# Low parts of weights and a norm's shift moved from GpSimd to VectorE in some stretches of a decoder trunk

## The chip, the cores and the metric

One core of a Trainium2 chip runs the whole kernel in one launch. The metric is device time in microseconds (us), the median of three runs.

## The reference

One inference step of a 4-layer decoder trunk, in float32, for two groups that share all weights: one prompt of 512 tokens and 8 sequences of 8 new tokens ("sample"). Layers 0 and 3 have a Conformer convolution as mixer, layer 1 a sparse attention with three branches, layer 2 a causal pooling; every layer ends in a gated feed-forward block with a 3-tap convolution.

```python
mod = silu(c) @ ada_w[i] + ada_b[i]; sh1, sc1, g1, sh2, sc2, g2 = split(mod, 6)
h = rms_norm(x, norm1_g[i]) * (1 + sc1) + sh1
x = x + g1 * mixer(h)                       # conv / attention / pooling
h = rms_norm(x, norm2_g[i]) * (1 + sc2) + sh2
x = x + g2 * conv_ffn(h)                    # 1024 -> 2 x 2816 -> 1024
```

## The kernel before, in words

Activations lie transposed: 128 of the 1024 features on the partitions, 8 such blocks (m), and two halves of the tokens (h), each 288 columns: 256 of the prompt and 32 of the sample. `x[h][q]` holds four blocks (q = 0, 1) of one half.

Every product runs in split precision. A weight block arrives by DMA in `raw` (128 x 2048); ScalarE writes its high part (a rounded copy, line 300 or 275), and another engine subtracts that from the raw weights to get the low part (line 305 or 276). TensorE then does three products per block: high by high (line 349), high weight by low activation (350), low weight by high activation (351). The activations of a norm, `h`, are split the same way (lines 640, 643, 650, 654).

The feed-forward blocks between the mixers are plain code: lines 275 and 276 split a whole weight block there, lines 357 to 360 are the products. What lies between two feed-forward blocks (the end of one, the norm, the mixer, the second norm, the start of the next) is a **flow**: a list of tasks, each with an engine, a duration, its dependencies, and counts of PSUM banks and slots. `Flow.run` is a list scheduler. At each step it takes, of all ready tasks, the one that can start earliest by the durations written in the code; ties go to the lower `prio`, then to the task that was added first. It issues the task at once, so the order of every engine's instructions is the order that it finds. A task may name two engines; the one on which it would end first is taken:

```python
e = min(range(len(eng)), key=lambda i: max(t, free.get(eng[i], 0.0)) + dur[i] + bias[i])
key = (max(t, free.get(eng[e], 0.0)), prio, n)
```

Here `t` is when the task's inputs are ready, `free` when the engine is. Nothing in it knows that VectorE and GpSimd may hinder each other.

There are five flows: layer 0 from the start (0 to about 330 us), the end of feed-forward 0 with the attention (about 630 to 1260), the end of feed-forward 1 with the pooling (about 1630 to 1760), the end of feed-forward 2 with layer 3's convolution (about 2130 to 2445), and the end of feed-forward 3 with the final norm (from about 2810). `Flow` is made with 18 slots, or with `slots=0` where `(l + 1) % 3 == 1`, which is the attention's flow (l = 0) and the last one (l = 3).

`w_tasks` adds the tasks that split a weight block in chunks of 512 columns: `hi` on ScalarE, `part` (line 305) on VectorE or GpSimd; after the last chunk it issues the load of the next block on SyncE's queue. It is called after the norm's tasks have been added.

`f_norm` works by half and by four blocks. For the sample's columns: `s_mul` (GpSimd, line 629), `s_rs` (VectorE, line 633), `s_add` (GpSimd, line 637: the shift), `s_hi` (ScalarE, line 640), `s_lo` (VectorE, line 643). For the prompt's, block by block: `p_mul` (VectorE, line 646), `p_hi` (ScalarE, line 650), `p_lo` (VectorE, line 654). Line 586 is the reciprocal of the norm's root on VectorE. Lines 498 to 500 are the residual `x + g * y`. `f_pool` has a shift of its own (line 1242) that the diff leaves alone.

Of the kernel before, what the change touches and what calls it, by code (L numbers as in the profile page):

```python
# [27 lines left out]
OP = mybir.AluOpType  # L28
# [73 lines left out]
class Flow:  # L102
# [5 lines left out]
    def __init__(self, banks=8, slots=18, warm=True):  # L108
        self.clock = dict(tick=0, warm=True, done=0.0) if warm else {}
        self.tasks = []  # L110
        self.banks, self.slots = banks, slots

    def add(self, eng, dur, fn, *deps, take=0, give=0, st=0, sg=0, prio=0, bias=(0, 0, 0)):


        if isinstance(eng, str):
            eng, dur = (eng,), (dur,)
        flat = []

        def walk(x):  # L120
            if isinstance(x, (list, tuple)):
                for y in x:
                    walk(y)
            elif x is not None:
                flat.append(x)
        walk(deps)
        self.tasks.append((eng, dur, fn, flat, (take, st), (give, sg), prio, bias))
        return len(self.tasks) - 1
# [64 lines left out]
class Trunk:  # L193
# [87 lines left out]
    def w_tasks(self, fl, tag, *deps, lo=("DVE", "POOL")):  # L281

        nc = self.nc
        n = self.nu
        self.nu += 1
        assert self.plan[n][0] == tag, (self.plan[n][0], tag)
        if n < self.ns:
            return (lambda: self.ws[n]), self.wt[n][1] if self.wt.get(n, (None,))[0] is fl else [None] * 4
        assert n == self.ns
        cs = range(0, self.plan[n][1], 512)  # L290
        self.ns += 1
        out, parts = [], set()
        a = None
        before = self.wt[n - 1][1] if self.wt.get(n - 1, (None,))[0] is fl else None

        def hi(c):
            if c == 0:
                self.ws[n] = self.wp.tile([128, 2, 2048], F32R, name="w", tag="w")
            sl = slice(c, min(c + 512, self.plan[n][1]))
            nc.scalar.activation(self.ws[n][:, 0, sl], self.raws[n][:, sl], AF.Copy)  # L300

        def part(c, eng):
            sl = slice(c, min(c + 512, self.plan[n][1]))
            w, r = self.ws[n], self.raws[n]
            self.eng(eng).tensor_tensor(w[:, 1, sl], r[:, sl], w[:, 0, sl], OP.subtract)  # L305
            parts.add(c)
            if len(parts) == len(cs):
                del self.raws[n]
                self.nr += 1
                self.w_dma()  # L310
        for c in cs:
            a = fl.add("ACT", 0.54, lambda c=c: hi(c), a, before, *[d(c) if callable(d) else d for d in deps])
            d = tuple({"DVE": 0.62, "POOL": 1.2}[e] for e in lo)
            out.append(fl.add(lo, d, (lambda e, c=c: part(c, e)) if len(lo) > 1 else (lambda c=c: part(c, lo[0])), a))
        out += out[-1:] * (4 - len(out))
        self.wt[n] = fl, out
        return (lambda: self.ws[n]), out
# [297 lines left out]
    def f_norm(self, fl, l, which, rs, ready, mdep=None):  # L615

        nc = self.nc
        B = self.modv(l, 3 * which)
        s0, S = self.f_scale(fl, l, which, mdep)
        t = {}  # L620
        self.hh, get = self.parts()

        def tt(h, q):
            if (h, q) not in t:
                t[h, q] = self.slot([128, 4, H], F32, name="nt")
            return t[h, q]

        def s_mul(h, q):
            nc.gpsimd.tensor_tensor(self.svq(tt(h, q)), self.svq(self.X[h][q]), self.bcq(S(), q, h), OP.mult)

        def s_rs(h, q):
            v = tt(h, q)[:, :, HP:H]
            nc.vector.tensor_tensor(v, v, rs[h][1]()[:, None, HP:H].to_broadcast([128, 4, H - HP]), OP.mult)

        def s_add(h, q):
            v = self.svq(tt(h, q))
            nc.gpsimd.tensor_tensor(v, v, self.bcq(B, q, h), OP.add)

        def s_hi(h, q):
            nc.scalar.activation(get(0, h, q)[:, :, HP:H], tt(h, q)[:, :, HP:H], AF.Copy)  # L640

        def s_lo(h, q):
            nc.vector.tensor_tensor(get(1, h, q)[:, :, HP:H], tt(h, q)[:, :, HP:H], get(0, h, q)[:, :, HP:H], OP.subtract)

        def p_mul(h, m):
            nc.vector.scalar_tensor_tensor(tt(h, m // 4)[:, m % 4, :HP], self.xv(h, m)[:, :HP], S()[:, m, 0:1],
                                           rs[h][1]()[:, :HP], op0=OP.mult, op1=OP.mult)

        def p_hi(h, m):
            nc.scalar.activation(get(0, h, m // 4)[:, m % 4, :HP], tt(h, m // 4)[:, m % 4, :HP], AF.Identity,  # L650
                                 bias=B[:, m, 0:1])

        def p_lo(h, m):
            nc.vector.scalar_tensor_tensor(get(1, h, m // 4)[:, m % 4, :HP], tt(h, m // 4)[:, m % 4, :HP], B[:, m, 0:1],
                                           get(0, h, m // 4)[:, m % 4, :HP], op0=OP.add, op1=OP.subtract)
        dep = {}
        for h in range(2):
            for q in range(2):
                ms = range(4 * q, 4 * q + 4)
                x = fl.add("POOL", 0.4, lambda h=h, q=q: s_mul(h, q), s0[q], [ready[h, m] for m in ms])  # L660
                x = fl.add("DVE", 0.25, lambda h=h, q=q: s_rs(h, q), x, rs[h][0])
                x = fl.add("POOL", 0.4, lambda h=h, q=q: s_add(h, q), x)
                a = fl.add("ACT", 0.25, lambda h=h, q=q: s_hi(h, q), x)
                b = fl.add("DVE", 0.2, lambda h=h, q=q: s_lo(h, q), a)
                for m in ms:
                    x = fl.add("DVE", 0.4, lambda h=h, m=m: p_mul(h, m), s0[m // 4], ready[h, m], rs[h][0])
                    x = fl.add("ACT", 0.41, lambda h=h, m=m: p_hi(h, m), x)
                    x = fl.add("DVE", 0.4, lambda h=h, m=m: p_lo(h, m), x)
                    dep[h, m] = [a, b, x]
        return dep  # L670
# [2076 lines left out]
```

## Time and profile before

| | us |
|---|---|
| median of three runs | 2862.21 |
| lowest, highest | 2859.83, 2865.05 |
| the profiled execution | 2859.49 |
| its span | 2857.7 |
| TensorE busy in it | 2754.8 |

TensorE's matmuls are named `pa`, `pb`, `pd` in the feed-forward blocks, `pc` where a norm's output is consumed first, `pd` also for a mixer's output projection, `pp` for the pooling's product, `adaps` for the modulation, `st` for the sums of a norm. Line 351 takes the low part of a weight, line 350 the low part of an activation.

### The profile page before, as it was taken

How to read it: one execution, taken by the hardware profiler on the slowest of the kernel's cores; microseconds unless marked ns; L12 is line 12 of the kernel's file. 1: busy time of each engine (PE TensorE's matmuls, PEld its weight loads, DVE VectorE, ACT ScalarE, POOL GpSimd, SP SyncE). 2: the span in 40 equal slices, each digit the busy share in tenths (PEclk: the TensorE clock that was granted, in tenths of full speed). 3: DMA queues.
4: the chain of work that ended last, by engine and by line, in shares of the span. 5: the costliest groups of instructions: out<-in, count | busy, mean ns of one | idle time of the engine just before them, and what ended most of it. 6: DMA issues, size and time to landing. Idle time of an engine off the chain costs nothing.

```text
span 2857.7 us, 50727 instructions
## 1 busy us (share of the span) xinstructions
PE 2754.8 (96%) x20677; PEld 2473.0 (87%) x20677; DVE 1598.2 (56%) x3437; ACT 978.8 (34%) x2094; POOL 505.8 (18%) x917
## 2 busy tenths in 40 slices
PE   7999999999999999989999979999999989999998
PEld 5667999999899656889999958999998758999997
DVE  5545644445736575464455686545557456645555
ACT  3124422222546565342222244222233134322223
POOL 2432200000434334010000052000003432000001
PEclk8999999999999999999999989999999999999999
DMA  8554243333443446224222269222233561222221
GB/s 313 174 172 171 89 148 145 136 133 133 147 155 134 138 155 234 88 97 148 97 89 74 97 198 139 74 89 89 83 111 115 163 236 45 85 78 89 89 76 64
DMA packets 105385, 363.88 MB, mean 127 GB/s; under 512 B 28128, under 2 KB 38272, under 8 KB 83904
## 3 DMA queue, kind: packets, MB, share of 16 engines
q1 hardware_dynamic: 97248, 344.50, 36.3%
q0 software_dynamic: 2816, 8.39, 0.9%
q10 hardware_dynamic: 5088, 7.74, 0.8%
q8 instruction: 163, 2.67, 0.4%
q14 instruction: 70, 0.57, 0.1%
HBM read 335.38 MB, written 22.80 MB: 125 GB/s over the span
## 4 chain that ended last, share of the span: by engine, by line
PE 86%; DVE 6%; DMA 4%; ACT 1%; issue 1%; SPq 1%; POOL 1%; ACTq 0%; DVEq 0%; POOLq 0%
PE pa L357 6%; PE pa L360 6%; PE pa L358 6%; PE pb L358 6%; PE pb L357 6%; PE pb L360 6%; PE pd L357 5%; PE pd L360 5%; PE pd L358 5%; PE pd L349 3%; PE pd L350 3%; PE pd L351 3%; PE adaps L421 2%; PE pts L953 2%; DMA ada<-in_ada_dram 2%; PE pc L350 2%
## 5 line engine op out<-in xcount | busy, mean ns | idle before, releaser
L276 DVE TENSOR_TENSOR w<-raw,w 128x2048 fp32r<-128x2048 f32 (+1 forms) x117 | 259.4, 2217 | 388.1 <-ACT w L275 388.1
L357 PE MATMUL pa<-h,w 128*128 128x288 f32 x1280 | 363.3, 299 | 5.6 <-ACT w L275 5.6
L358 PE MATMUL pa<-h,w 128*128 128x288 f32 x1280 | 360.4, 296 | 0.0
L358 PE MATMUL pb<-h,w 128*128 128x288 f32 x1216 | 341.6, 295 | 0.0
L357 PE MATMUL pb<-h,w 128*128 128x288 f32 x1216 | 341.5, 296 | 0.0
L357 PE MATMUL pd<-u,w 128*128 128x288 f32 x1152 | 323.5, 296 | 0.0
L358 PE MATMUL pd<-u,w 128*128 128x288 f32 x1152 | 322.9, 295 | 0.0
L740 POOL COPY so<-ab 128x2 f32<-128x2 f32 x88 | 17.0, 193 | 1518.5 <-ACT ab L710 1518.5
L275 ACT ACTIVATE w<-raw 128x2048 fp32r<-128x2048 f32 (+1 forms) x117 | 218.9, 1871 | 176.4 <-PE pd L360 176.4
L360 PE MATMUL pa<-h,w 128*128 128x288 f32 x1280 | 274.9, 296 | 1.0 <-DVE w L276 1.0
L357 PEld LDWEIGHTS pa<-h,w 128*128 128x128 f32 x1280 | 241.8, 189 | 24.3 <-issue 16.8
L360 PE MATMUL pb<-h,w 128*128 128x288 f32 x1216 | 259.8, 295 | 0.0
L360 PE MATMUL pd<-u,w 128*128 128x288 f32 x1152 | 247.0, 296 | 0.0
L358 PEld LDWEIGHTS pa<-h,w 128*128 128x128 f32 x1280 | 242.1, 189 | 0.0
L358 PEld LDWEIGHTS pb<-h,w 128*128 128x128 f32 x1216 | 229.0, 188 | 0.0
L357 PEld LDWEIGHTS pb<-h,w 128*128 128x128 f32 x1216 | 228.7, 188 | 0.0
L357 PEld LDWEIGHTS pd<-u,w 128*128 128x128 f32 x1152 | 216.8, 188 | 6.7 <-issue 6.7
L358 PEld LDWEIGHTS pd<-u,w 128*128 128x128 f32 x1152 | 216.8, 188 | 0.0
L498 DVE TENSOR_TENSOR rtmp<-pd,mod 128x32 f32<-128x32 f32 x368 | 68.5, 186 | 261.6 <-PE pd L360 174.9
L305 DVE TENSOR_TENSOR w<-raw,w 128x512 fp32r<-128x512 f32 (+1 forms) x203 | 166.2, 859 | 84.2 <-ACT w L300 83.4
L720 ACT ACTIVATE ab<-ab 128x576 f32<-128x576 f32 x88 | 60.4, 687 | 435.2 <-DVE ab L739 435.2
L360 PEld LDWEIGHTS pa<-h,w 128*128 128x128 f32 x1280 | 205.9, 189 | 1.5 <-DVE w L276 1.3
(359 smaller groups left out, 6502.6 us busy)
## 6 DMA issues: line engine op xcount, KB each, us to landing
raw<-in_w_dram SPq DMA_DIRECT2D x165, 1024.0 KB
ada<-in_ada_dram SPq DMA_DIRECT2D x192, 512.0 KB
xs<-ub SPq DMA_DIRECT2D x56, 270.0 KB
raw<-in_w_dram SPq DMA_DIRECT2D x16, 768.0 KB
x<-in_x_dram SPq DMA_DIRECT2D x8, 576.0 KB
xsp<-x SPq DMA_DIRECT2D x8, 576.0 KB
x<-xsp SPq DMA_DIRECT2D x8, 576.0 KB
out_wo_dram<-in_sw_dram SPq DMA_DIRECT2D x8, 512.0 KB
```

The lines of the kernel that those rows point to most:

```text
L275: nc.scalar.activation(w[:, 0, :width], r[:, :width], AF.Copy)
L276: self.lo_eng.tensor_tensor(w[:, 1, :width], r[:, :width], w[:, 0, :width], OP.subtract)
L305: self.eng(eng).tensor_tensor(w[:, 1, sl], r[:, sl], w[:, 0, sl], OP.subtract)
L349: nc.tensor.matmul(ps[:, :H], hi, mv(k, 0, h), start=first, stop=False)
L350: nc.tensor.matmul(ps[:, :H], hi, mv(k, 1, h), start=False, stop=False)
L351: nc.tensor.matmul(ps[:, :H], lo, mv(k, 0, h), start=False, stop=last)
L357: nc.tensor.matmul(ps[h][:, :H], hi, mv(k, 0, h), start=first, stop=False)
L358: nc.tensor.matmul(ps[h][:, :H], hi, mv(k, 1, h), start=False, stop=False)
L360: nc.tensor.matmul(ps[h][:, :H], lo, mv(k, 0, h), start=False, stop=last)
L421: nc.tensor.matmul(self.a_ps[32 * j:32 * j + 32, 0:N], self.cm[:, k, :], raw[j * N // 1024][:, j * N % 1024:j * N % 1024 + N], start=(k == ...
L498: nc.vector.tensor_tensor(t, self.sv(ps), self.bc(G, m, h), OP.mult)
L720: self.nc.scalar.activation(acc, acc, AF.Silu)
```

## The change

`Flow` gets a flag `busy`, true where `slots == 0`. In the other flows a low part is planned with 0.68 us on VectorE and 2.6 us on GpSimd in place of 0.62 and 1.2, and `s_add` of `f_norm` is a VectorE task of 0.28 us in place of a GpSimd task of 0.4.

```diff
+        self.busy = slots == 0
...
-            d = tuple({"DVE": 0.62, "POOL": 1.2}[e] for e in lo)
+            d = tuple(({"DVE": 0.62, "POOL": 1.2} if fl.busy else {"DVE": 0.68, "POOL": 2.6})[e] for e in lo)
...
-        def s_add(h, q):
+        def s_add(h, q, e):
             v = self.svq(tt(h, q))
-            nc.gpsimd.tensor_tensor(v, v, self.bcq(B, q, h), OP.add)
+            self.eng(e).tensor_tensor(v, v, self.bcq(B, q, h), OP.add)
...
-                x = fl.add("POOL", 0.4, lambda h=h, q=q: s_add(h, q), x)
+                e = "POOL" if fl.busy else "DVE"
+                x = fl.add(e, 0.4 if fl.busy else 0.28, lambda h=h, q=q, e=e: s_add(h, q, e), x)
```

## Rows read from the trace of the kernel before

**Rows 1.** The page's part 1: busy us (share of the span) xinstructions, by engine.

```profile
PE 2754.8 (96%) x20677; PEld 2473.0 (87%) x20677; DVE 1598.2 (56%) x3437; ACT 978.8 (34%) x2094; POOL 505.8 (18%) x917
```

**Rows 2.** Windows: length, busy us (xinstructions) by engine, PEclk, DMA share, GB/s.

```profile
1650.00:1760.00 110.00, 89.11 (x569) 63.59 (x567) 91.41 (x207) 49.52 (x116) 56.22 (x92) 0.91 0.92 169
...
2440.00:2800.00 360.00, 360.00 (x2716) 359.85 (x2716) 189.86 (x405) 98.77 (x154) 10.71 (x82) 1.00 0.24 83
```

**Rows 3.** Waits of PE, whole span: total us, times, longest us.

```profile
PE pc L350 <- DVE h L643: 9.1, 4, 3.7
```

**Rows 4.** Waits of PE, 240 to 330 us; 2400 to 2440 answers the same row.

```profile
PE pc L350 <- DVE h L654: 2.2, 2, 1.4
```

**Rows 5.** Lines 305, 637, 633: count, ns min/median/max; the POOL rows by flow.

```profile
L305 DVE TENSOR_TENSOR w<-raw,w x203: 559/685/2808, 23.6 to 2820.3; 128x512 fp32r<-128x512 f32 x101, 128x384 fp32r<-128x384 f32 x1
L305 POOL TENSOR_TENSOR w<-raw,w x14: 1266/1464/2245, 44.3 to 310.6; 128x512 fp32r<-128x512 f32 x14
L305 POOL TENSOR_TENSOR w<-raw,w x13: 1267/1299/1627, 1631.5 to 1727.7; 128x512 fp32r<-128x512 f32 x13
L305 POOL TENSOR_TENSOR w<-raw,w x20: 1262/1456/2218, 2129.2 to 2426.9; 128x512 fp32r<-128x512 f32 x20
L637 POOL TENSOR_TENSOR nt<-nt,mod x28: 418/528/593, 26.1 to 2432.9; 128x128 f32<-128x128 f32 x28
L633 DVE TENSOR_TENSOR nt<-nt,rstd x28: 275/279/1442, 25.5 to 2432.5; 128x128 f32<-128x128 f32 x28
```

**Rows 6.** Timeline of DVE from 2157 us (start us, us, engine line op xcount), layer 3's norm.

```profile
2157.92 1.43 DVE L633 TENSOR_TENSOR nt<-nt,rstd 128x128 f32<-128x128 f32 x1
2159.27 3.90 DVE L646 SCALAR_TENSOR_TENSOR nt<-x,nS,rstd 128x256 f32<-128x256 f32 x4
...
2164.37 1.24 DVE L500 TENSOR_TENSOR x<-x,rtmp 128x32 f32<-128x32 f32 x1
...
2166.13 0.28 DVE L643 TENSOR_TENSOR h<-nt,h 128x128 fp32r<-128x128 f32 x1
...
2184.41 0.86 DVE L646 SCALAR_TENSOR_TENSOR nt<-x,nS,rstd 128x256 f32<-128x256 f32 x2
```

**Rows 7.** Timeline of POOL in the same stretch.

```profile
2157.91 1.29 POOL L305 TENSOR_TENSOR w<-raw,w 128x512 fp32r<-128x512 f32 x1
...
2159.98 2.90 POOL L305 TENSOR_TENSOR w<-raw,w 128x512 fp32r<-128x512 f32 x2
```

**Rows 8.** Timeline of PE in the same stretch, idle before in brackets.

```profile
2166.46 0.61 PE L350 MATMUL pc<-h,w 128*128 128x288 f32 x1 [3.67 <-DVE h L643]
```

**Rows 9.** Windows: PE just after that wait, columns as in Rows 2.

```profile
2166.46:2169.47 3.01, 3.01 (x15) 2.73 (x19) 3.01 (x9) 2.21 (x5) 1.76 (x3) 0.50 0.99 280
```

**Rows 10.** Timeline of DVE, then of POOL, 295 to 302 us: layer 0's second norm.

```profile
296.43 2.46 DVE L646 SCALAR_TENSOR_TENSOR nt<-x,nS,rstd 128x256 f32<-128x256 f32 x3
298.81 1.37 DVE L643 TENSOR_TENSOR h<-nt,h 128x128 fp32r<-128x128 f32 x1
300.11 1.49 DVE L646 SCALAR_TENSOR_TENSOR nt<-x,nS,rstd 128x256 f32<-128x256 f32 x1
...
297.13 4.18 POOL L305 TENSOR_TENSOR w<-raw,w 128x512 fp32r<-128x512 f32 x3
```

**Rows 11.** Timelines of ACT, DVE and POOL in the pooling flow.

```profile
1659.02 1.16 ACT L300 ACTIVATE w<-raw 128x512 fp32r<-128x512 f32 x2 [1.27 <-issue]
...
1699.01 0.42 DVE L1290 TENSOR_TENSOR pw<-hp 128x262 f32<-128x262 f32 x1
1699.36 0.68 DVE L305 TENSOR_TENSOR w<-raw,w 128x512 fp32r<-128x512 f32 x1
...
1705.23 1.49 DVE L1290 TENSOR_TENSOR pw<-pw 128x264 f32<-128x264 f32 x1
...
1704.96 1.47 POOL L305 TENSOR_TENSOR w<-raw,w 128x512 fp32r<-128x512 f32 x1
```

**Rows 12.** The chain that ended last, 1704 to 1760 us: start us, us, what.

```profile
1711.23 32.62 DMA out_ps_dram<-hs
```

## The prediction

> **What bounds the kernel now.** I read the page's busy times first: TensorE is busy 2754.8 of 2857.7 us [rows 1], so nothing can be won but its idle 103 us and what it does at a low clock. Then the windows: a feed-forward stretch shows TensorE busy for all of its 360 us [rows 2], so a flow that hands over one microsecond earlier ends the kernel one microsecond earlier, and no engine but TensorE matters there. So I look only at what TensorE waits for inside the three flows that the change reaches (layer 0, pooling, layer 3). The attention's flow keeps the old figures, and so does the last one, since its l is 3 and it too is made with `slots=0`.
>
> TensorE's waits name two places with a norm in front: in layer 3's first norm the second matmul on `pc` waits 3.67 us for line 643 on VectorE [rows 3, 8], and in each of the two second norms (layers 0 and 3) two matmuls wait 2.2 us for line 654, the longer one 1.4 [rows 4]. What makes VectorE late there shows when the timelines of VectorE and GpSimd are laid side by side. A scale step of line 646 takes 0.40 us from start to start when GpSimd is quiet (two took 0.86) [rows 6]. While a low part (line 305) runs on GpSimd, one VectorE instruction stretches until it is over: line 633 took 1.43 us instead of 0.28, line 646 took 1.49, line 643 took 1.37 instead of 0.28 [rows 5, 6, 10]. Four of line 646 took 3.90 us where 0.47 + 3 x 0.40 = 1.67 is the quiet figure: 2.23 us lost beside two low parts that took 2.90 [rows 6, 7]. So a low part on GpSimd costs a busy VectorE 1.0 to 1.15 us. On VectorE itself it costs 0.62 from start to start (0.69 with its pipeline's end; the median is 0.685) [rows 5, 11].
>
> The Trainium skill, SBUF — State Buffer, section Who interferes with whom, says that a VectorE instruction with two SBUF inputs and a GpSimd instruction that reads SBUF exclude each other, whichever starts second waiting in full. The trace agrees for the rows just named. It also says that the lock works both ways, which speaks against the change: each low part on VectorE would hold up GpSimd's tasks. By the skill's rule the sum below would lose up to 0.6 us for each place where GpSimd is the later engine; in the rows of the norms GpSimd then has only these low parts and shifts.
>
> **The change, part by part.** On GpSimd stand 14, 13 and 20 low parts in the three flows, 47 of them, at medians of 1.46, 1.30 and 1.46 us [rows 5]. Of line 637's 28 instructions four belong to each of seven norms; five norms lie in these flows, so 20 move, at 0.53 us.
>
> *How many low parts really move.* The planner compares ends. With the old figures GpSimd is taken as soon as VectorE would be free 0.58 us later than the task could start on GpSimd (1.2 - 0.62); with the new ones at 1.92 us (2.6 - 0.68). A low part is added after the norm's tasks and loses every tie to them, so in a norm, where VectorE has 7 to 9 us of ready work, it is passed over until VectorE is 1.92 us ahead and then still goes to GpSimd, at its early place. The next one must wait for GpSimd's planned 2.6 us, so about two of four stay there and two fall to VectorE behind the norm. I take two of four in saturated stretches, and all elsewhere. That deferral is real shows in the pooling flow: two chunks' high parts ran from 1659.02 on, and a low part of theirs came at 1699.36 on VectorE [rows 11].
>
> *The second norms of layers 0 and 3.* Before the first product can go on, VectorE's instructions are stretched by low parts of which the last three took 4.18 us on GpSimd [rows 10]. Two fewer beside them gives 2 x 1.05 = 2.1 us back; the shift, now on VectorE, costs about 0.2 (line 633, of the same shape, takes 0.28, and 0.2 from start to start). So the activations are ready 1.9 us earlier, more than the 1.4 us that TensorE waits: the first wait goes, 1.4. Of the second wait (2.2 - 1.4 = 0.8) I take half, since two low parts now stand on VectorE (1.24 us) where two stretches were (2.1). Together 1.8 us in each, 3.6 for both. The most that can be won is 2.2 each; the loss is bounded by the second rival below.
>
> *Layer 3's first norm.* VectorE loses 1.15 us (line 633), 2.23 (line 646) and some 1.0 (line 500: 1.24 for 32 columns, where 128 take line 643 0.28) ahead of line 643, 4.4 us in all [rows 6]. Two of four low parts gone gives 2.1 back, the shift takes 0.2: 1.9 us of the wait of 3.67 [rows 8]. After that wait TensorE's granted clock is 0.50, the lower of its two levels (1.2 GHz), and 15 instructions take 3.01 us [rows 9]; before it TensorE stood still for 3.67 us. If a shorter wait keeps the clock, those instructions alone get half of their time back, 1.5 us. I take 1.0 of it. Together 2.9, between 0 and 5.2.
>
> *The pooling flow.* VectorE and GpSimd are both full here; TensorE has 89.1 us of 110 and a mean clock of 0.91 [rows 2]. One low part on GpSimd at 1704.96 stretches line 1290 from 0.42 to 1.49 us [rows 11]; as a VectorE instruction it would cost 0.62, so 0.45 is won on each of the two last ones of the pooling's weight: 0.9. What is won after 1711 us is worth nothing: there the chain goes through an output transfer of 32.62 us [rows 12], which ends at 1743.85, and the next feed-forward block's start waits for it. The planner will also pick other engines for the many tasks here that may run on either; that is worth -3 to +4 us, by TensorE's idle 21 us there, of which I let a fifth move. Value taken: 0.9.
>
> *The rest costs nothing.* The two low parts of each feed-forward tail and those in the tails of the convolutions lie beside a TensorE that has no wait for lines 305 or 643 there; were that cover gone, each would cost its 0.62. The shift's 0.2 us on VectorE in the halves that come second are covered by TensorE's queue of the first half. Low parts on VectorE free the raw buffer at another time, and with it the load of the next block on SyncE's queue; the next use is a whole block of products away. The scalar engine gets nothing.
>
> *The sum.* 3.6 + 2.9 + 0.9 = 7.4 us, from the profiled execution's 2859.5 (span 2857.7 and 1.8 outside it) to 2852.1. That execution was 2.7 us below the median of 2862.2, so the forecast on the median is 2854.8.
>
> **The rivals.**
>
> *Won time is hidden.* The transfers decide: the output transfer in the pooling flow, and layer 3's low clock stays because TensorE still stands still. Then only the second norms' 3.6 us are left and a little of the rest is lost: 2858.6 on the median. For it: a single transfer is 32.62 us of the chain [rows 12]. Against it: the norms' waits name VectorE and no transfer [rows 3, 4].
>
> *The low parts wait on VectorE.* This is the other side. The point from which it decides is the 1.92 us: if the low part that TensorE needs first is planned on VectorE (ready a little before it is free, so that GpSimd is never 1.92 us better), it stands behind the whole half of the norm. In the second norms that is 16 x 0.40 for lines 646 and 654, five sample steps of 0.2 and its own 0.62, 8.0 us from line 646's first at 296.43, or 304.4, where the last stretched step ended at 301.60 and, with one line 654 behind it, TensorE went on at 302.0 [rows 10]: 2.4 us more, twice. In layer 3's first norm 6.4 + 1.2 + 0.62 = 8.2 from 2157.92, 2166.1 against 2166.46 [rows 6, 8]: no change, but residuals of the other half stand between, so 1.0 more. With 0.9 more in the pooling flow, 6.7 us: 2868.9. For it: the 40 us between 1659.02 and 1699.36 [rows 11]. Against it: the rule of ends as worked out above.
>
> *The change doesn't do what it says.* In the saturated stretches GpSimd keeps nearly all low parts; what moves stood under cover. Then only the shift changes, 0 to -1 us: 2861.5. For it: passed-over tasks go to GpSimd by the rule. Against it: GpSimd's planned 2.6 us keep the second and third of them off it.
>
> **How the numbers follow.** Forecast 0.46, hidden 0.20, low parts that wait on VectorE 0.22, little moved 0.12. About 0.2%, 5.7 us, is what a measurement of this kernel tells from no change: faster means under 2856.5, slower over 2867.9. The forecast is faster in 0.42 of its 0.46, the hidden case in 0.04 of 0.20, the last in 0.02 of 0.12: 0.48. The waiting low parts are slower in 0.20 of 0.22 and the last case in 0.02: 0.22. The rest, 0.30, is within. The forecast's own range is 2851.7 (4.4 + 5.2 + 0.9 won) to 2858.6 (the second norms alone). The range for all cases goes down to 2847 (the same with the pooling flow's 4 instead of 0.9 gives 2848.6, and the cover of the rest may be thinner than I think) and up to 2868, near the slower case.
>
> **What would show it.** Right: line 305 on GpSimd falls from 47 in these flows to some 10 to 20; in the second norms TensorE's wait of 1.4 us for line 654 is gone, and line 646 shows at most two stretches over 1 us ahead of it; in layer 3's first norm the wait of 3.67 is under 2 and the low clock after it is shorter. Wrong: TensorE waits for line 305 (`pc L351 <- DVE w L305`) in the norms, or the low parts are still on GpSimd at the same places. The forecast fails altogether if the pooling flow, where the order is least bound, moves by more than 4 us either way.

## The result, and the profile after

After the change the kernel takes 2902.42 us (median of 4 runs, 2897.82 to 2905.2), against 2862.07 (4 runs): a ratio of 1.0141, with a 95% interval of 1.0128 to 1.0154. It is 40 us slower; 2854.8 was forecast, and the range ended at 2868. The profiled execution has a span of 2901.5 us, 43.8 more than before.

The page's part 1 first, the columns of [rows 1]:

```profile
PE 2770.3 (95%) x20677; PEld 2473.3 (85%) x20677; DVE 1597.0 (55%) x3476; ACT 981.2 (34%) x2093; POOL 476.3 (16%) x879
```

GpSimd lost 29.5 us of work and VectorE gained none, though 17 low parts and 20 shifts were moved to it. Together they take 25.7 us there, 12.1 of them the shifts, which at 0.28 us each would be 5.6; other lines of VectorE took as much less. TensorE has the same 20677 instructions and 15.5 us more of busy time at a mean granted clock of 0.978 instead of 0.985, so part of the loss is a lower clock and the rest, 28 us, is standing still. An engine's total says nothing of where.

The moves fell short of the forecast, in number and above all in place. These are line 305 (now 307) on GpSimd by flow and line 637 (now 639) on VectorE, columns as in [rows 5]:

```profile
L307 POOL TENSOR_TENSOR w<-raw,w x10: 1277/1402/2243, 44.0 to 326.3; 128x512 fp32r<-128x512 f32 x10
L307 POOL TENSOR_TENSOR w<-raw,w x5: 1294/1442/1682, 1726.1 to 1747.2; 128x512 fp32r<-128x512 f32 x5
L307 POOL TENSOR_TENSOR w<-raw,w x15: 1269/1342/2209, 2181.0 to 2469.4; 128x512 fp32r<-128x512 f32 x15
L639 DVE TENSOR_TENSOR nt<-nt,mod x20: 277/280/1379, 26.3 to 2474.5; 128x128 f32<-128x128 f32 x20
```

47 low parts on GpSimd became 30, and 20 shifts moved. The shift's maximum of 1379 ns is new: it is now itself a VectorE instruction that stands beside a low part, and six of the 20 took 1.35 to 1.38 us.

In the norms of layers 0 and 3, where VectorE is full, nearly all low parts stayed on GpSimd. These are layer 0's second norm and layer 3's first, each in before and then in after:

```profile
L305 POOL TENSOR_TENSOR w<-raw,w x7: 1295/1467/1494, 295.0 to 310.6; 128x512 fp32r<-128x512 f32 x7
L307 POOL TENSOR_TENSOR w<-raw,w x6: 1277/1402/1477, 310.8 to 326.3; 128x512 fp32r<-128x512 f32 x6
L305 POOL TENSOR_TENSOR w<-raw,w x7: 1262/1452/1477, 2157.9 to 2174.6; 128x512 fp32r<-128x512 f32 x7
L307 POOL TENSOR_TENSOR w<-raw,w x7: 1271/1327/1462, 2181.0 to 2203.3; 128x512 fp32r<-128x512 f32 x7
```

With layer 0's first norm (3 and 2) and layer 3's second (7 and 6) these four norms have 24 before and 21 after. Of the 17 that moved, 3 stood in them, 8 in the pooling flow and 6 elsewhere.

To find the 40 us I cut the span into stretches that hold the same TensorE work in both kernels, and compared lengths. The columns are those of [rows 2]. Of before, the convolution stretches of layer 0 and layer 3, and the pooling flow:

```profile
51.80:237.00 185.20, 177.40 (x1589) 124.97 (x1592) 88.43 (x122) 40.97 (x83) 71.50 (x58) 0.98 0.62 209
...
1630.00:1761.00 131.00, 110.11 (x728) 83.93 (x728) 106.49 (x245) 60.48 (x139) 59.77 (x97) 0.92 0.87 165
...
2181.90:2365.90 184.00, 176.39 (x1596) 132.62 (x1595) 98.82 (x144) 52.38 (x111) 72.98 (x66) 0.99 0.52 175
```

The same work in after:

```profile
54.20:251.40 197.20, 180.39 (x1590) 126.70 (x1592) 86.53 (x120) 40.63 (x82) 69.89 (x56) 0.96 0.60 198
...
1647.60:1786.20 138.60, 114.60 (x727) 84.58 (x727) 104.41 (x257) 60.57 (x140) 45.90 (x83) 0.88 0.85 155
...
2207.10:2407.10 200.00, 181.79 (x1596) 131.24 (x1595) 96.67 (x146) 51.89 (x107) 73.77 (x63) 0.97 0.49 166
```

The two convolution stretches are 12.0 and 16.0 us longer, the pooling flow 7.6. VectorE is busy 2 us less in each of the three than before, and GpSimd at most 0.8 us more. With the first norms (+2.4 and +2.1) and the second norms (+2.2 and +3.7) the list reaches 46; what lies between these stretches gives 2 back. Each length comes from one trace. In kernels that leave these stretches as in before, the second norms agree within some tenths of a microsecond, but a convolution stretch was up to 2.5 us longer, so 1 or 2 us in a convolution say little.

What TensorE waits for in layer 3's convolution stretch, before and then after (total us, times, longest):

```profile
PE adaps L421 <- DMA ada<-in_ada_dram: 4.5, 3, 3.0
PE st L542 <- POOL y L1112: 1.9, 1, 1.9
```

```profile
PE adaps L423 <- DMA ada<-in_ada_dram: 11.5, 4, 8.0
PE pts L956 <- DMA xs<-ub: 5.5, 3, 2.8
```

Both are transfers: `ada`, the modulation's weights, and `xs`, the shifted inputs of the convolution's taps. No low part and no shift is named. Why a transfer is late is read on SyncE's queue beside TensorE. Of before, the load (start, length of its issue) and the product that waits for it:

```profile
2304.48 4.26 SPq L391 DMA_DIRECT2D ada<-in_ada_dram  x2
...
2320.71 1.05 PE L421 MATMUL adaps<-ada,cm 128*32 128x512 f32 x4 [1.34 <-DMA ada<-in_ada_dram]
```

Of after:

```profile
2345.41 4.47 SPq L393 DMA_DIRECT2D ada<-in_ada_dram  x2
...
2360.85 2.75 PE L423 MATMUL adaps<-ada,cm 128*32 128x512 f32 x6 [7.96 <-DMA ada<-in_ada_dram]
```

From issue to use it is 16.23 us before and 15.44 after: the load is no slower. What differs is what TensorE has to do meanwhile. Windows of these two stretches with the products on `pc` alone, before and then after:

```profile
2304.48:2320.71 16.23, 10.05 (x72) 9.58 (x72) 0.95 (x4) 0.69 (x2) 1.00 0.57 151
```

```profile
2345.41:2360.85 15.44, 3.43 (x24) 3.20 (x24) 0.95 (x4) 0.00 (x0) 0.87 0.53 158
```

72 products were left to cover the load before, 24 after: 6.62 us of cover gone, and 0.79 us of TensorE's other work with them. The load was 0.79 us shorter, so the wait grew by 6.62 us (7.96 - 1.34). The other 48 products had been issued earlier, because the planner's order has changed: between two groups of taps stood 96 products before, where after has 192 products and then two groups of taps together (64 taps, 128 instructions). The tap groups in after also meet their `xs` late, by the order for the same reason, though the cover of these loads was not counted; the clock falls behind the second wait:

```profile
2272.09 1.05 PE L956 MATMUL pts<-xs,dg 128*32 128x512 f32 x2 [0.24 <-DMA xs<-ub]
2275.95 16.79 PE L956 MATMUL pts<-xs,dg 128*32 128x512 f32 x122 [2.81 <-DMA xs<-ub]
```

**Theory (order).** The new figures change the order that the planner finds for every engine of the three flows, far from the edited tasks, and this order leaves TensorE without work while loads are on their way. **Rival (load).** The work given to VectorE delays what follows it there, and the rest is a consequence.

### The profile page after: what moved, and what is told of

It is laid out like the page before. It is cut to its first block, busy times and chain, and to the rows that moved or that the text cites. A ratio compares the mean times of both kernels' runs of the same rounds, so it can differ in the third digit from the quotient of the medians.

```text
span 2901.5 us, 50753 instructions
## 1 busy us (share of the span) xinstructions
PE 2770.3 (95%) x20677; PEld 2473.3 (85%) x20677; DVE 1597.0 (55%) x3476; ACT 981.2 (34%) x2093; POOL 476.3 (16%) x879
## 4 chain that ended last, share of the span: by engine, by line
PE 84%; DMA 7%; DVE 6%; issue 1%; POOL 1%; ACT 1%; SPq 1%; DVEq 0%; POOLq 0%; ACTq 0%
PE pa L359 6%; PE pa L362 6%; PE pa L360 6%; PE pb L360 6%; PE pb L359 6%; PE pb L362 6%; PE pd L359 5%; PE pd L362 5%; PE pd L360 5%; DMA ada<-in_ada_dram 3%; PE pts L956 3%; PE pd L351 3%; PE pd L352 3%; PE pd L353 3%; PE adaps L423 2%; DMA xs<-ub 2%
## 5 line engine op out<-in xcount | busy, mean ns | idle before, releaser
L307 DVE TENSOR_TENSOR w<-raw,w 128x512 fp32r<-128x512 f32 (+1 forms) x220 | 178.6, 854 | 99.4 <-ACT w L302 98.6
L302 ACT ACTIVATE w<-raw 128x512 fp32r<-128x512 f32 (+1 forms) x265 | 151.4, 621 | 162.6 <-issue 44.8
```

## The experiments

All compared with runs of before on the same chip, 2859 to 2860.5 us. "Before's order" means that every engine's program stands in before's order but for the moved instructions, which keep their place in the list of issue. Texts of mine that say 28 shifts count all seven norms; 20 move. The 27 low parts of the first text are 47, and the 2.9 us that a later one gives as the most for a low part on GpSimd were two of them; the longest single one took 2.25.

| kernel | median, us | ratio (95%) |
|---|---|---|
| before's order, all low parts and shifts of the three flows on VectorE | 2849.0 | 0.9963 (0.9949 to 0.9977) |
| the same, shifts left on GpSimd | 2847.76 | 0.9963 (0.9949 to 0.9977) |
| the same with shifts on VectorE, and all other low parts too | 2845.9 | 0.9948 (0.9932 to 0.9965) |
| before's order, after's engines | 2863.71 | 1.0016 (1.0007 to 1.0026) |
| after's order, before's engines | 2898.48 | 1.0127 (1.0110 to 1.0144) |
| new figures of the low parts only | 2896.59 | 1.0132 (1.0115 to 1.0149) |
| shift only | 2867.93 | 1.0028 (1.0015 to 1.0040) |
| change in the pooling flow only | 2865.63 | 1.0021 (1.0011 to 1.0031) |
| after, tap loads planned at 7.0 | 2894.52 | 1.0118 (1.0101 to 1.0135) |
| before, tap loads planned at 6.5 | 2873.08 | 1.0044 (1.0028 to 1.0061) |
| before without the modulation's later loads | 2842.13 | 0.9936 (0.9919 to 0.9952) |
| after without them | 2864.16 | 1.0018 (1.0008 to 1.0027) |
| low parts planned at 0.64 and 1.2 | 2858.79 | 0.9995 (0.9985 to 1.0004) |
| low parts planned at 0.68 and 1.38 | 2887.62 | 1.0094 (1.0078 to 1.0111) |
| re-planned with all low parts on VectorE | 2901.12 | 1.0138 (1.0118 to 1.0158) |

Length in us of the stretches with the same TensorE work, from windows as above:

| stretch | before | after | before's order, all on VectorE | before's order, after's engines | after's order, before's engines | re-planned, all on VectorE |
|---|---|---|---|---|---|---|
| layer 0, first norm | 13.9 | 16.3 | 12.3 | 14.9 | 14.3 | 15.1 |
| layer 0, convolution | 185.2 | 197.2 | 185.0 | 184.8 | 198.7 | 180.7 |
| layer 0, second norm | 93.9 | 96.1 | 93.3 | 96.0 | 95.8 | 102.3 |
| pooling flow | 131.0 | 138.6 | 129.4 | 130.5 | 138.6 | 148.2 |
| layer 3, first norm | 25.0 | 27.1 | 22.8 | 24.7 | 25.0 | 38.0 |
| layer 3, convolution | 184.0 | 200.0 | 185.0 | 185.4 | 201.0 | 182.0 |
| layer 3, second norm | 82.0 | 85.7 | 78.2 | 84.1 | 83.8 | 92.4 |

**1. The swap with the order kept.** The planner gets before's figures, and only the issuing engine differs:

```diff
-            out.append(fl.add(lo, d, (lambda e, c=c: part(c, e)) if len(lo) > 1 else ...
+            out.append(fl.add(lo, d, (lambda e, c=c: part(c, e if fl.busy else "DVE")) if len(lo) > 1 else ...
-                x = fl.add("POOL", 0.4, lambda h=h, q=q: s_add(h, q, "POOL"), x)
+                x = fl.add("POOL", 0.4, lambda h=h, q=q: s_add(h, q, "POOL" if fl.busy else "DVE"), x)
```

> Before's figures and so before's order of issue on every engine; in the three flows each low part that the order puts on GpSimd, and each shift, is issued on VectorE at the same place. Order theory (the 40 us come from the new order of the products and taps, not from the engine): the two convolution stretches are back at before's time (28 us less than after), the pooling flow within 3 us of before's, the second norms keep their 1.4 to 1.8 us each: 2850 to 2868 us. Load theory (work that VectorE takes over delays what follows it there): 27 low parts at 0.69 to 1.38 us and 28 shifts at 0.3 us or more stay on VectorE, so most of the 40 us stay: 2885 us or more.

2849.0 us, 11 faster than before and just under the range. VectorE carries more here than in after, and both convolution stretches are as short as before's within 1 us, so the load theory falls for them.

**2. The square of order and engines.** One kernel has before's order and after's engine for each single low part and shift, the other the reverse: the list of issue by the one set of figures, the engine out of a table made from the other kernel.

```diff
+LOW = {1: (0, 1), 9: (0, 1), ...}    # weight block: chunks on GpSimd
+            go = "POOL" if c // 512 in LOW.get(n, ()) else "DVE"
-            out.append(fl.add(lo, d, (lambda e, c=c: part(c, e)) ...
+            out.append(fl.add(lo, d, (lambda e, c=c, go=go: part(c, e if fl.busy else go)) ...
```

> One cell of a square of order and engines: every instruction in before's order, but each low part and each shift on the engine that after gives it (30 low parts on GpSimd instead of 47, the 28 shifts on VectorE). Order theory: no loss, near the kernel that took all of them to VectorE: 2847 to 2860 us. Load theory: after's engines bring after's loss: 2890 us or more.

> The opposite cell: every instruction in after's order, but each low part and each shift on the engine that before gives it (47 low parts and the 28 shifts on GpSimd). Order theory: as slow as after or slower, since the parts now also lack VectorE's speed: 2900 to 2920 us. Load theory: VectorE has before's load, so 2858 to 2872 us.

After's engines in before's order cost 4.7 us (my 2847 to 2860 missed it: I had expected some gain); after's order on before's engines costs 39.4, nearly all of the loss (2898.48, just under the range that I had given it). In the table its convolution stretches and its pooling flow are after's. The order is the cause of nearly all of the loss; what after's engines cost stands in the norms, and experiment 6 comes back to it.

**3. The parts of the change.**

```diff
# low parts only: the shift is a GpSimd task of 0.4 again
+                x = fl.add("POOL", 0.4, lambda h=h, q=q: s_add(h, q, "POOL"), x)
# shift only: the low parts by the old figures
+            d = tuple({"DVE": 0.62, "POOL": 1.2}[e] for e in lo)
# pooling only: in the flows with a convolution
+            fl.busy = True
```

> The new figures of the low parts alone; the shift stays on GpSimd at 0.4. TensorE's order in this kernel has layer 0's convolution batched as after (192 products, 64 taps, twice) and layer 3's in small batches as before. Order theory: layer 0's stretch loses about 12 us as after, layer 3's none (15.6 us less than after): 2875 to 2888 us. Load theory: the low parts hold nearly all the time that moves to VectorE, so 2893 to 2902 us, and layer 3's stretch is as long as after's.

> The shift alone on VectorE (28 of 0.28 us, planned as 0.28), the low parts by the old figures. TensorE's order in both convolutions is before's. Order theory: both stretches at before's time, a few tenths of a microsecond per half in the norms either way: 2857 to 2867 us. Load theory: the shift stands in the chain of each half's sample part, stretched to 1.4 us beside a low part on GpSimd: 2867 to 2880 us.

> The change in the pooling flow alone; layers 0 and 3 keep before's figures. If the parts of the change add up, this one costs what after's trace shows between the pooling flow's start and the attention that follows, 7.6 us, less 2 us in the feed-forward tail: 2866 to 2871 us. If instead the pooling flow loses only because it starts from another state of the queues (a later transfer), it comes back to 2860 to 2864 us.

The low parts' figures alone give 36.6 us, more than the order theory's 2875 to 2888 and within the load theory's range; by its place it still spoke against load: layer 3's convolution, whose order stayed in small groups, lost only 2.3 us, layer 0's 17, the pooling flow 14 (a single wait for a load of `ada` there is 15.0 us long). So the parts don't add up: each set of figures gives another order, with its loss at another place. The shift alone gave 2867.93, just outside the one range and at the low end of the other: layer 0's convolution as long as before (order theory), 3.1 us more in the first norm ahead of it, where a shift took 1.35 us beside a low part (load theory), and 3.0 in layer 3's convolution (neither). For the 40 us this one decides nothing. The pooling flow alone lost 5.6 us, what after's trace shows there with the feed-forward tail (7.6 - 2).

**4. One planned figure, no change of engines.** The time from a tap load's issue to its landing, 6.0 in both kernels:

```diff
-                    xs.append(fl.add("XQ", 6.0, lambda: None, x))
+                    xs.append(fl.add("XQ", 7.0, lambda: None, x))    # in after; 6.5 in before
```

> After with one planned figure changed, the time from a tap load's issue to its landing, 7.0 instead of 6.0. Engines and figures of the change stay. In the order that results the middle of both convolution stretches reads 144 products, 32 taps, 48 products, 32 taps, 144 products, 32 taps instead of 192, 64, 192, 64. If the batches make the loss of the two stretches, some 20 to 28 us come back: 2874 to 2884 us. If the loss is in the loads of the modulation's weights at the stretch's end whatever the batches (waits of 7.68, 3.16, 7.96, 1.39 and 1.83 us in after), 12 us or less come back: 2890 us or more.

> Before with the same planned figure at 6.5 instead of 6.0; the change itself is not made. In the order that results layer 0's convolution reads 192 products, 64 taps, twice, as in after, and layer 3's stays in small batches. If that order costs by itself, layer 0's stretch is 8 to 14 us longer and the whole 2868 to 2876 us. If it takes the change's engines or its norms to make it slow, 2857 to 2864 us.

In before, 0.5 us in a planned figure cost 14 us: this order loses by itself, on before's engines. In its trace (a span 17.0 us longer) layer 0's batched stretch is 15.7 us longer, and layer 3's 6.4, though that one kept its small batches; the text foresaw nothing there. In after, breaking the batches brought back some 5 to 8 us and not 20 to 28, as the text's second reading has it, and not in the convolutions. Both stretches stayed as long (199.2 and 199.6 us), with other waits: the longest are 5.0 us for `ada`, 4.9 for the modulation's row (`mrow`) and 4.7 for a low part on VectorE. The second norms became 3.4 and 6.1 us shorter. So "the batches of 192 products and 64 taps" is too narrow a cause. The last kernel of experiment 7 has this one's small batches in layer 0 and took 180.7 us there, so the size of the batches alone decides neither way: it is the order as a whole.

**5. The loads taken away.** The modulation's products from the 17th step on read a constant that is in SBUF already:

```diff
     def ada_load(self):
+        if n >= 16:
+            self.a_raw[n] = [self.par, self.par]
+            self.a_n += 2
+            return
```

> Leaves out the loads of the modulation's weights but for the first 16 steps: the later products read a constant tile that is in SBUF already (so the modulations of all but the first are of other numbers). Order and all else as before. By before's waits for these loads (2.03 us in layer 0's stretch, 1.34 and 3.04 in layer 3's) and some at the end of the attention: 2840 to 2856 us. It is the base for the next kernel.

> The same loads left out of after; order and all else as after. Cover theory (the new order leaves TensorE without work while loads are on their way): the waits of 7.68, 3.16, 7.96, 1.39, 1.83 us in the two stretches and of 6.7 us in the pooling flow go, and the distance to the kernel before without these loads shrinks from 40 us to some 15 to 25 us; what is left is the taps' loads, the norms and the pooling flow's last wait. Rival (the loads only stand in front of other late work, such as the late parts on VectorE): the distance stays at 33 us or more.

The distance between the two orders falls from 40 to 22.0 us, within the cover theory's range. By stretch, before and after without the loads: layer 0's convolution 179.9 and 184.7, the pooling flow 128.5 and 129.6, layer 3's convolution 179.1 and 186.8. So in the two convolutions 15.5 of the 28 us hang on the modulation's loads. The pooling flow's 6.5 can't be read in this way: without the loads other waits stand there (22.5 us for `mrow` in after's order, 10.3 for a pooled activation in before's). Leaving out the loads also takes their traffic away (133 GB/s where before had 175 in layer 3's convolution), so this shows that the loss hangs on these loads; that missing cover is the reason rests on the load counted out above. The windows of layer 3's convolution without them, before's order and then after's:

```profile
2172.10:2351.20 179.10, 174.39 (x1597) 131.44 (x1596) 98.18 (x144) 52.73 (x111) 74.15 (x66) 0.99 0.41 133
```

```profile
2180.70:2367.50 186.80, 177.68 (x1596) 130.26 (x1595) 98.25 (x145) 51.87 (x107) 74.56 (x63) 0.98 0.41 133
```

Of the 7.7 us left, 3.3 are busy time at a lower clock; the waits that remain there are nearly all for `xs` (7.9 us; none in before's order). That these too would go if the taps' loads came earlier was not tried.

**6. Which part of the swap wins.**

```diff
# shifts stay on GpSimd
+                x = fl.add("POOL", 0.4, lambda h=h, q=q: s_add(h, q, "POOL"), x)
# or: all other low parts to VectorE too
+            out.append(fl.add(lo, d, (lambda e, c=c: part(c, "DVE")) if len(lo) > 1 else ...
```

> Before's order; all low parts of the three flows on VectorE, the shifts on GpSimd as before. If the 11 us that the swap of both won come from GpSimd's low parts (each up to 2.9 us, and stretching VectorE's work beside them), most of it stays: 2848 to 2854 us. If the shift off GpSimd was what won: 2857 to 2862 us.

> Before's order; all low parts on VectorE, those of the attention's flow too (15 of them), the shifts of the three flows on VectorE. The attention's first norm and its products were not late on low parts in the trace of before, so VectorE's extra 10 us there lie beside TensorE's work: within 3 us of the kernel that left them on GpSimd, 2846 to 2852 us. If VectorE is short there: 2853 to 2860 us.

With the low parts on VectorE the shift is worth nothing either way; the low parts win it all. The version with all of them on VectorE has the lowest ratio, 0.9948, though the intervals of the three overlap; all three beat before and after.

Why does moving 17 of the low parts (with the shifts) cost 4.7 us and moving all 47 win 11? The win shows in the timelines of layer 3's first norm. With before's order and after's engines, VectorE and then GpSimd (lines 646, 637 and 305 of before are 652, 643 and 310 in this kernel, 648, 639 and 307 in the next):

```profile
2156.47 4.36 DVE L652 SCALAR_TENSOR_TENSOR nt<-x,nS,rstd 128x256 f32<-128x256 f32 x3
2160.76 0.28 DVE L643 TENSOR_TENSOR nt<-nt,mod 128x128 f32<-128x128 f32 x1
...
2156.26 4.29 POOL L310 TENSOR_TENSOR w<-raw,w 128x512 fp32r<-128x512 f32 x3
```

With before's order, all low parts on VectorE and the shifts on GpSimd:

```profile
2148.51 0.47 DVE L648 SCALAR_TENSOR_TENSOR nt<-x,nS,rstd 128x256 f32<-128x256 f32 x1
2148.91 0.90 DVE L307 TENSOR_TENSOR w<-raw,w 128x512 fp32r<-128x512 f32 x1
2149.73 1.27 DVE L648 SCALAR_TENSOR_TENSOR nt<-x,nS,rstd 128x256 f32<-128x256 f32 x3
```

Three scale steps took 4.36 us beside three low parts on GpSimd, and 1.27 without. A low part among them cost VectorE 0.82 us from start to start. So each one on GpSimd beside a full VectorE costs (4.36 - 1.27) / 3 = 1.0 us, and 25 of the 30 that after left there stand in the norms.

The loss shows in the second norms. With before's order and after's engines, TensorE's waits for line 654 [rows 4] fall from 2.2 to 0.5 us in layer 0's, but a new one of 2.16 us comes, for the sums of the next half. From that kernel VectorE, ScalarE and TensorE, and last ScalarE in before:

```profile
304.96 1.37 DVE L643 TENSOR_TENSOR nt<-nt,mod 128x128 f32<-128x128 f32 x1
306.37 0.31 ACT L646 ACTIVATE h<-nt 128x128 fp32r<-128x128 f32 x1 [0.70 <-DVE nt L643]
307.77 0.51 ACT L656 ACTIVATE h<-nt,mod 128x256 fp32r<-128x256 f32 x1 [1.10 <-DVE nt L652]
308.19 0.39 ACT L575 ACTIVATE stsb<-st 128x288 f32<-128x288 f32 x1
308.63 1.33 PE L540 MATMUL st<-stsb,comb 128*128 128x288 f32 x2 [2.16 <-ACT stsb L575]
...
306.27 0.39 ACT L569 ACTIVATE stsb<-st 128x288 f32<-128x288 f32 x1
```

The shift (line 643), now on VectorE, took 1.37 us beside a low part on GpSimd. ScalarE's next instructions in order wait for it and for the scale step behind it, and `stsb`, which stands behind them, comes at 308.19 instead of 306.27. TensorE's busy time in this norm also grew by 1.5 us (granted clock 0.98 instead of 1.00). Layer 3's second norm has the same wait, and the kernel with the shift only has one of 1.6 us in both; with shifts and all low parts on VectorE no such wait is over 0.5. So the shift costs where low parts stay on GpSimd beside it. A kernel in before's order that moves the shift alone was not run.

**7. Other figures, and the swap re-planned.**

```diff
-            d = tuple(({"DVE": 0.62, "POOL": 1.2} if fl.busy else {"DVE": 0.68, "POOL": 2.6})[e] for e in lo)
+            ... else {"DVE": 0.64, "POOL": 1.2} ...     # near; shift on GpSimd
+            ... else {"DVE": 0.68, "POOL": 1.38} ...    # as measured; shift on GpSimd
+            ... else {"DVE": 0.68, "POOL": 90.0} ...    # all on VectorE; shift on VectorE
```

> Low parts in the three flows planned at 0.64 us on VectorE and 1.2 on GpSimd instead of 0.62 and 1.2; shifts on GpSimd as before. TensorE's order in both stretches is close to before's (layer 0's alike, layer 3's six products earlier). If any new order loses: 2866 us or more. If only the order that the figure 2.6 brings loses: 2856 to 2864 us.

> The same with the durations of the trace, 0.68 and 1.38 us. Layer 0's convolution comes out batched as in after, layer 3's stays in batches of 96 products and 32 taps. If the batched order loses whatever the figure: layer 0's stretch some 12 us longer, 2870 to 2880 us. If truer figures give a better order: 2850 to 2860 us.

> After with GpSimd's figure so high that the planner puts each low part of the three flows on VectorE; shifts on VectorE. Engines as in the order-kept swap that took 11 us off, in an order of the planner's own. If the order is what counts: it loses some of these 11 us or more, 2855 to 2880 us. If engines count as well as order, and the order is only bad where GpSimd's parts are late: 2845 to 2852 us.

The near figures give nearly before's order and no difference. The measured ones, though truer, lose 27 us, more than either range: 9.6 in layer 0's batched convolution, 18.9 in the pooling flow, where one wait for a load of `ada` is 21.9 us long. The third is the plainest: the engines of experiment 1, where the order was kept and 11 us were won, and with the planner's own order 41 us lost, again more than either range. Here the loss is not in the convolutions (180.7 and 182.0 us) but in the norms and the pooling flow. TensorE's waits from the pooling flow to the last norm, and then the low parts in layer 3's first norm on VectorE's timeline:

```profile
PE adaps L423 <- DMA ada<-in_ada_dram: 31.9, 15, 20.7
PE pc L353 <- DVE w L307: 22.6, 2, 11.7
```

```profile
2199.85 1.27 DVE L656 SCALAR_TENSOR_TENSOR h<-nt,mod,h 128x256 fp32r<-128x256 f32 x3
2201.04 4.89 DVE L307 TENSOR_TENSOR w<-raw,w 128x512 fp32r<-128x512 f32 x8
```

The wait of 20.7 us is for one load of `ada` at the end of the pooling flow, which is 17 us longer than before's. In layer 3's norms the low parts stand behind the whole norm, since in the list they come after its tasks; TensorE waited 11.7 us for them in the first and 11.0 in the second. In experiment 1 they stand between the scale steps, at the places that GpSimd's tasks had.

## Why the prediction was wrong

The step that failed is **"The rest costs nothing"**. It looked for low parts and shifts among TensorE's waits in the convolutions and the feed-forward tails and found none, which was true, and is true of after. But it took the order of all the other instructions as given. The same prediction knew that the planner "will also pick other engines for the many tasks here", and gave this -3 to +4 us in the pooling flow alone. In a list scheduler every later choice hangs on the planned times so far, so two changed figures moved products, taps and loads that name neither. In the convolutions TensorE then waited mostly for loads with too little work left to cover them. The two convolution stretches hold 28 of the 44 us.

- *How many low parts really move*: two of four in full norms. Wrong: 21 of 24 stayed in the norms of layers 0 and 3, and 30 in all, where 10 to 20 were written. This was one of the prediction's own signs of being wrong ("still on GpSimd at the same places"), and of the moves, though not of the time, its third rival was right ("GpSimd keeps nearly all low parts", 0.12).
- *The second norms*, 1.8 us won in each. Wrong: 2.2 and 3.7 lost. The wait of 1.4 us for line 654 [rows 4] did shrink, to 1.24, but waits for the high part and the sample's low part stand beside it. With before's order and after's engines these norms also lose (96.0 and 84.1 against 93.9 and 82.0), so here the engines count. There the waits for line 654 did fall by 1.7 us, near the 1.8 forecast; the term that failed is the shift, put at 0.2 us, which was itself stretched to 1.37 beside a low part and brought the new wait of 2.16 us. With no low part on GpSimd the norms won 0.6 and 3.8. The mechanism, a low part on GpSimd that costs a full VectorE 1.05 us, was right; it was not applied to the shift. Whether half of the low parts off would give half of the gain was not tested, since half never left.
- *Layer 3's first norm*, 2.9 won. 2.1 were lost, with all seven low parts still on GpSimd. The wait of 3.67 us [rows 3, 8] is gone, and three others came in its place:

```profile
2192.12 0.75 PE L536 MATMUL st<-stsb,comb 128*128 128x288 f32 x2 [1.45 <-ACT stsb L571]
...
2197.22 0.40 PE L352 MATMUL pc<-h,w 128*128 128x288 f32 x1 [1.24 <-DVE h L656]
2199.70 0.51 PE L351 MATMUL pc<-h,w 128*128 128x288 f32 x1 [1.56 <-ACT h L642]
```

  With before's order and all on VectorE 2.2 us were won. That is near 2.9 by luck: 2.9 was worked out for two of four low parts gone, and here all were.
- *The pooling flow*, 0.9 won; the forecast was to fail altogether if this flow "moves by more than 4 us either way": it moved by 7.6. The output transfer of [rows 12] is not slower; in the new order ScalarE meets it in the middle of the second norm (so too in the kernel with the change in the pooling flow only, where TensorE then waits 5.2 us). ScalarE's waits in after from 1735 to 1765 us, and then the chain there:

```profile
ACT h L652 <- DMA out_ps_dram<-hs: 10.2, 1, 10.2
```

```profile
1727.62 32.01 DMA out_ps_dram<-hs
1759.70 0.51 ACT h L652
```

  The norm's `h` waits for a buffer that this transfer still reads (`h` and `hs` are slots of one pool), and TensorE waits 5.8 us for that norm. In before no instruction of a norm waited for it on ScalarE; the feed-forward's start did (line 710, 2.4 us), and TensorE lost 0.95 there. The transfer stood in [rows 12] as a cover ("what is won after 1711 us is worth nothing"); that it could also become a wait in the norm was not asked.
- *The rivals.* The slower side came true, but by none of the three mechanisms at the size given, and no rival had the order of the other instructions. "The low parts wait on VectorE" (6.7 us) is not what after's trace shows: its longest wait for line 307 is 2.8 us, in the pooling flow, where before has one of 2.6. It is real in the re-planned kernel of experiment 7, and there larger than priced: 11.7 and 11.0 us in layer 3's norms, where the prediction had 1.0 and 2.4.

That the forecast of 7.4 us won is near what the full swap wins with the order kept (11 us) is in part luck: it was worked out for about half of the norms' low parts, and after's own engines with the order kept lose 4.7 us. The trace of before could show the price of a low part; it could not show what order the planner would find.

## What to carry to other kernels

Where a planner writes the order of instructions, a change of its figures is a change of the whole schedule: before pricing the edited instructions, list which others change place, and price the cover of each load that they cover. To move work between engines, keep the order and change only who executes it, then measure; here that is 11 to 13 us faster where all low parts move, 4.7 slower where a part of them moves with the shifts, and the engines of the first re-planned 41 slower. And truer durations for single tasks need not give a better plan: here they cost 27 us. That this comes from what the plan leaves out (the engines' mutual hindrance, the time that loads really take) is likely but was not tested.

## What the runs showed of the hardware

A two-input VectorE instruction beside a reading GpSimd one waits in full and repeatedly: three scale steps of 0.47 us took 1.45 each while three low parts ran, and ended 0.28 us after the last of them (2156.47 + 4.36 against 2156.26 + 4.29). The Trainium skill, SBUF — State Buffer, section Who interferes with whom, says that the two exclude each other; this trace agrees. Its practical side was unexpected in size: in before's order, with the shifts on VectorE, all 47 low parts there too are 15 us faster than 17 there and 30 on GpSimd (0.9963 against 1.0016).

A wait can be paid twice, by the clock, and its length alone doesn't tell whether it is. Two groups of taps in after, of layers 0 and 3, in windows:

```profile
129.40:143.30 13.90, 13.90 (x123) 4.06 (x123) 11.33 (x15) 0.60 (x1) 6.50 (x8) 1.00 0.64 201
2275.95:2292.70 16.75, 16.75 (x123) 4.28 (x123) 8.81 (x14) 0.60 (x1) 8.09 (x9) 0.83 0.71 213
```

The first came behind a wait of 2.92 us for `xs` and kept the full clock; the second came behind 2.81 us, with 0.24 us of another wait shortly before, and a part of it ran at the lower of the two levels (1.2 GHz): 2.85 us more for the same instructions.
